# Order of the weight sums, the combine passes and the activation sums in the MLP stage of a decoder layer

## Chip, cores and metric

One core of one Trainium2 chip. The metric is the device time of one execution in microseconds (us), median of several runs. One launch computes the whole layer.

## What is computed

One layer of a hybrid decoder, in float32: an input projection, dilated window attention in three groups, a gated mixing of positions, an output projection with residual, and a squared-ReLU MLP. All that the change touches lies in the MLP, on N = 512 + 32 = 544 token columns, with D = 2048 and an inner width of 8192:

```python
h2 = rms_norm(x, norm_ffn)
x = x + jnp.square(jax.nn.relu(h2 @ w_up)) @ w_down
```

## The kernel before

Activations are kept transposed, features on the 128 partitions and tokens along the free axis; NH = 272 is half of the tokens. Every float32 operand is split into a high part (a cast to the matmul's float32 type, on ScalarE, ACT) and a low part (the difference, on VectorE, DVE), and a product is three matmuls: high times high, high times low, low times high (L903 to L905, on TensorE, PE).

The MLP's products are done by a scheme of Strassen's kind: a 2 × 2 block product with seven block products for eight. It needs sums of four weight blocks ahead of the matmuls, sums of four activation blocks likewise, and a combination of the seven results behind them.

**Units and stretches.** The MLP is a loop over 256 units (L888), 128 of `w_up` and then 128 of `w_down`. A unit is one weight load of 512 KB (`raw`, three buffers, issued on SyncE's queue, SP) and 42 matmuls of 272 columns: seven products × two halves j × three. Four units (g = 0 to 3) accumulate into the same seven PSUM tiles `qs[1]` to `qs[7]`; they make a stretch s, of which there are 32 up and 32 down. `qs[1]` and `qs[2]` lie in one tile `pt` (`pa`), `qs[6]` and `qs[7]` in another (`pb`), the rest in one each. The products of a unit go in the order 1, 2, 6, 7, 5, 4, 3.

**What a unit issues, in program order** (L888 to L907): the load of the raw weights of unit u+3; `prepare()` (L721) for unit u+1; the hooks of (s, g); its own 42 matmuls; and in g = 3 the end of the stretch. Each engine runs its instructions in that order.

**prepare** makes the sums `vs` (L733 two blocks, L735 and L736 one each, every one from the one before), casts the raw blocks and the sums to `vh` (ACT: L732 and L737) and makes the differences `vl` (DVE: L738 and L739). `vs`, `vh` and `vl` have two buffers each, so the casts for unit u+1 wait until PE has left unit u−1.

**End of a stretch.** `combine` (L763) copies `qs[1]` to SBUF (ACT, L765) and makes four results out of the seven tiles in seven DVE passes (L766 to L772). PE's first matmul of the next stretch overwrites `qs[1]`.

**Up** (`up_out`, L818): the result tile `f` gets a ReLU and a square on ACT in g = 1 of the next stretch (L823, L824), then in g = 2 its three sums (`sums`, L682: L683 to L685) and a store to DRAM `rd` by GpSimd's queue (POOL, L828).

**Down** (`down_out`, L859): the results go by an accumulating DMA to DRAM `yd` (POOL, L864). In g = 1 of each down stretch one activation tile of the following stretches is loaded from `rd` into `tl` (POOL, L838), in g = 2 it is split (`down_terms`: ACT L843, DVE L844). Around the turn from up to down, in stretches 31 and 32, nine such tiles are loaded and split. In the last eight stretches the finished sums are loaded, scaled (L848) and stored. `scale_back` (stretches 2 to 4) makes row factors, among them two reciprocals; in eight up stretches (8, 10, .. 22) L813 scales a part of the residual into `yd`.

Of the kernel before, what the change touches and what calls it, by code (L numbers as in the profile page):

```python
# [23 lines left out]
N = NP_ + NS  # L24
NH = N // 2
# [13 lines left out]
VB = 2 * P  # L39
# [4 lines left out]
def halves(t):  # L44
    return t.rearrange("p (a b) -> p a b", a=2)
# [7 lines left out]
def hybrid_layer_kernel(ctx, tc, xT, w_in, w_out, w_up, w_down, kc1, kc23, vc1, vc23, gains, biasp,  # L53
                        biass, gw, gws, gb, consts, y, kout, vout, gvout):
    nc = tc.nc
    V, A, G, S = nc.vector, nc.scalar, nc.gpsimd, nc.sync
# [12 lines left out]
    def load(src):  # L69
        raw = wp.tile([P, 8, P], F32, name="raw", bufs=3)  # L70
        S.dma_start(out=raw, in_=src)
        return raw

    def split_half(raw, j, copy=A.copy):
        wh = sp.tile([P, 4, P], F32R, name="wh", bufs=AHEAD + 1)
        wl = sp.tile([P, 4, P], F32R, name="wl", bufs=AHEAD + 1)
        r = raw[:, 4 * j:4 * j + 4, :]
        copy(wh, r)  # L78
        V.tensor_tensor(wl, r, wh.bitcast(F32), op=OP.subtract)  # L79
        return wh, wl  # L80
# [80 lines left out]
    def vtile():  # L161
        return ap.tile([P, N], F32, name="v", bufs=2)
# [7 lines left out]
    ssq = ap.tile([P, N], F32, name="ssq", tag="ss")  # L170

    pts = [main_psum() for _ in range(2)]
    raws = {}
# [26 lines left out]
    for c in range(4):  # L200
# [5 lines left out]
        w1 = split_half(raws[1, c // 2], c % 2, copy=V.tensor_copy)  # L206
# [29 lines left out]
    def quad(dst, src):  # L236
        for a in range(4):
            for b in range(4):
                G.tensor_copy(dst[32 * a:32 * a + 32, b:b + 1], src[32 * b:32 * b + 32, a:a + 1])
# [6 lines left out]
    class Head:  # L246
# [260 lines left out]
    i = 0  # L507
    for h in range(NHEAD):
# [9 lines left out]
        for g in range(NG):  # L518
            pt = in_tile(i)
            i += 1  # L520
            t = vtile()
# [96 lines left out]
    ssq = vtile()  # L618
# [7 lines left out]
    for f in range(4):  # L626
        pt = in_tile(i)
        i += 1
        u = vtile() if f == 2 else zt[4 + f % 2]
# [5 lines left out]
    for part in range(2):  # L635
        if part:
            plan.drain()
        for pt in pts:
            if not part:
                plan.step()  # L640
            w = stream.get(load, split_half)
# [13 lines left out]
    ssq = tp.tile([P, N], F32, name="ssq1")  # L655
# [25 lines left out]

    def sums(f):  # L682
        V.tensor_tensor(f[:, 0:2, :], f[:, 7:8, :].to_broadcast([P, 2, NH]), f[:, 4:7:2, :], op=OP.subtract)  # L683
        V.tensor_tensor(f[:, 2, :], f[:, 6, :], f[:, 0, :], op=OP.subtract)
        V.tensor_tensor(f[:, 3, :], f[:, 5, :], f[:, 2, :], op=OP.subtract)  # L685

    def split_terms(k, f):
# [3 lines left out]
    def terms(k):  # L691
        f = xp.tile([P, 8, NH], F32, name="f")
        for dst, m in ((f[:, 4:8:3, :], k), (f[:, 5:7, :], k + PAIRS)):
            V.scalar_tensor_tensor(dst, halves(x1[m]), gn[:, 16 + m:17 + m], halves(rb), op0=OP.mult, op1=OP.mult)
        sums(f)
        split_terms(k, f)

    for m in M_ORDER[:2]:
# [14 lines left out]
    mix.close()  # L713

    uw = ctx.enter_context(tc.tile_pool(name="uw", bufs=1, side="right", reuse_waits="tile"))
    raws = []

    def fetch(src):
        raws.append(load(src))

    def prepare():  # L721
        raw = raws.pop(0).rearrange("p a b -> p (a b)")
        vs = uw.tile([P, 4 * VB], F32, name="vs", bufs=2)
        vh, vl = (uw.tile([P, 7 * VB], F32R, name=n, tag=n, bufs=2) for n in ("vh", "vl"))

        def part(t, i):
            return t[:, i * VB:(i + 1) * VB]

        def pair(t):
            return t.rearrange("p (a b) -> p a b", a=2)  # L730

        A.copy(vh[:, :3 * VB], raw[:, VB:])  # L732
        V.tensor_tensor(pair(vs[:, :2 * VB]), raw[:, None, :VB].to_broadcast([P, 2, VB]), pair(raw[:, VB:3 * VB]),  # L733
                        op=OP.add)
        V.tensor_tensor(part(vs, 2), part(vs, 1), part(raw, 1), op=OP.add)  # L735
        V.tensor_tensor(part(vs, 3), part(vs, 2), part(raw, 3), op=OP.add)  # L736
        A.copy(vh[:, 3 * VB:], vs)  # L737
        V.tensor_tensor(vl[:, :3 * VB], raw[:, VB:], vh[:, :3 * VB].bitcast(F32), op=OP.subtract)  # L738
        V.tensor_tensor(vl[:, 3 * VB:], vs, vh[:, 3 * VB:].bitcast(F32), op=OP.subtract)  # L739
        return vh, vl  # L740

    th.append(uw.tile([P, 7, NH], F32R, name="th7", tag="th7"))
    tl.append(uw.tile([P, 7, NH], F32R, name="tl7", tag="tl7"))
    units = [w[i] for w in (w_up, w_down) for i in range(w.shape[0])]
    for i in range(3):
        fetch(units[i])
    ready = [prepare()]
    terms(PAIRS - 1)
    tmp.close()
    yp = ctx.enter_context(tc.tile_pool(name="yp", bufs=1, reuse_waits="tile"))  # L750
# [3 lines left out]
    qs = {n: t[:, :NH] for n, t in ((1, pa[:, 0]), (2, pa[:, 1]), (6, pb[:, 0]), (7, pb[:, 1]), (5, q5), (4, q4),  # L754
                                     (3, q3))}
# [5 lines left out]
        return yp.tile([P, 8, NH], F32, name="f", bufs=2)  # L761

    def combine(c11, c12, c21, c22):  # L763
        w = yp.tile([P, NH], F32, name="w", bufs=2)
        A.copy(w, qs[1])  # L765
        V.tensor_tensor(c11, qs[2], w, op=OP.add)  # L766
        V.tensor_tensor(w, qs[6], w, op=OP.subtract)
        V.tensor_tensor(c21, qs[7], w, op=OP.add)
        V.tensor_tensor(w, qs[5], w, op=OP.add)
        V.tensor_tensor(c22, qs[5], c21, op=OP.add)  # L770
        V.tensor_tensor(c21, qs[4], c21, op=OP.add)
        V.tensor_tensor(c12, qs[3], w, op=OP.subtract)  # L772

    hooks = {}

    def hook(s, g, fn, *args):
        hooks.setdefault((s, g), []).append(partial(fn, *args))

    back = yp.tile([P, N], F32, name="back")

    def scale_back():
        o = out_tile()
# [35 lines left out]
    def up_out(p):  # L818
        f = term_tile()
        combine(f[:, 4, :], f[:, 7, :], f[:, 5, :], f[:, 6, :])  # L820

        def square():
            A.activation(f[:, 4:, :], f[:, 4:, :], AF.Relu)  # L823
            A.activation(f[:, 4:, :], f[:, 4:, :], AF.Square)  # L824

        def rest():
            sums(f)
            G.dma_start(out=rd[p], in_=f[:, :7, :])  # L828

        hook(p + 1, 1, square)  # L830
        hook(p + 1, 2, rest)

    def load_terms(n):
        k = n % PAIRS
# [42 lines left out]
    last, first = UPG - 1, UPG  # L877
# [9 lines left out]

    for u in range(len(units)):  # L888
        s, g = divmod(u, 4)
        if u + 3 < len(units):  # L890
            fetch(units[u + 3])
        if u + 1 < len(units):
            ready.append(prepare())
        for fn in hooks.get((s, g), []):
            fn()
        vh, vl = ready.pop(0)
        t0 = max(s - UPG, 0)
        for n, (v, t) in TERMS.items():
            for j in range(2):
                k = (t0 + 2 * g + j) % PAIRS  # L900
                c = slice(v * VB + j * P, v * VB + (j + 1) * P)
                first, last = g + j == 0, g + j == 4
                mm(qs[n], vh[:, c], th[k][:, t, :], start=first, stop=False)  # L903
                mm(qs[n], vh[:, c], tl[k][:, t, :], start=False, stop=False)  # L904
                mm(qs[n], vl[:, c], th[k][:, t, :], start=False, stop=last)  # L905
        if g == 3:
            up_out(s) if s < UPG else down_out(s - UPG)  # L907
# [198 lines left out]
```

## Time and profile before

| | us |
|---|---|
| median of 3 runs | 2199.11 |
| lowest and highest run | 2193.5, 2201.91 |
| profiled execution, device time | 2193.06 |
| span of its trace | 2191.3 |
| busy in the span: PE | 2096.3 (96%) |
| busy: DVE | 1754.9 (80%) |
| busy: ACT | 929.9 (42%) |
| busy: POOL | 234.5 (11%) |

The span goes from the first to the last instruction of one profiled execution. Matmuls overlap, and one is busy until its modelled end, so a share of PE near 100% means a gapless stream. The mean granted clock of TensorE is 0.987 of full speed. An arrow in a row names what ended an engine's idle time ahead of an instruction.

### The profile page before, as it was taken

Reading aid. Unit: us, or ns where it says so; the run is one execution under the profiler, and the core shown is the slowest. Engines: PE = TensorE matmul, PEld = TensorE weight load, DVE = VectorE, ACT = ScalarE, POOL = GpSimd, SP = SyncE. Lnnn points to the kernel's source line nnn. Section 1 sums busy time; section 2 is a strip of 40 time slices with the busy share of each in tenths; the row PEclk is TensorE's granted clock in tenths of the full one; section 3 lists DMA queues with packets and bytes.
Section 4 is the critical chain, followed back from the end, with each engine's and each line's share of the span. In section 5 each row is a group of like instructions: output and inputs, shape, how many; then the busy total and the mean of one; then the engine's idle time right before and its main releaser. Section 6 shows DMA issues by size and latency. Waiting matters only on the chain.

```text
span 2191.3 us, 40901 instructions
## 1 busy us (share of the span) xinstructions
PE 2096.3 (96%) x16392; PEld 2063.7 (94%) x16392; DVE 1754.9 (80%) x3566; ACT 929.9 (42%) x1296; POOL 234.5 (11%) x534
## 2 busy tenths in 40 slices
PE   8999999999899889999999999998999999999997
PEld 8999989899898889999999999998999999999997
DVE  5356767666687779989999998889888888898997
ACT  5334242332633344444444444455444444444442
POOL 3121120211211100000000000010000000000111
PEclk9999999999999999999999999999999999999999
DMA  5365665656564424454554544464655555565665
GB/s 190 97 192 185 209 194 190 207 181 197 179 200 131 158 94 150 145 170 165 179 179 163 181 154 148 159 261 140 185 152 182 153 181 168 173 181 155 205 212 156
DMA packets 109695, 378.13 MB, mean 173 GB/s; under 512 B 12640, under 2 KB 12752, under 8 KB 109504
## 3 DMA queue, kind: packets, MB, share of 16 engines
q1 hardware_dynamic: 81744, 243.58, 34.2%
q0 software_dynamic: 27760, 131.94, 19.7%
q8 instruction: 128, 2.10, 0.4%
q14 instruction: 63, 0.52, 0.1%
HBM read 305.87 MB, written 69.21 MB: 171 GB/s over the span
## 4 chain that ended last, share of the span: by engine, by line
PE 47%; issue 31%; DVE 8%; DMA 7%; ACT 3%; POOL 2%; SPq 0%; POOLq 0%; DVEq 0%; ACTq 0%
PE pt L87 14%; PE pt L903 6%; PE pt L905 6%; PE pt L904 6%; DMA kv<-in_kc_dram 4%; PE sm L903 2%; PE po L903 2%; PE sm L904 2%; PE po L904 2%; PE sm L905 2%; PE ms L904 2%; PE ms L903 2%; PE ms L905 2%; PE po L905 1%; POOL yd L864 1%
## 5 line engine op out<-in xcount | busy, mean ns | idle before, releaser
L903 PE MATMUL pt<-th,vh 128*128 128x272 f32 x2048 | 598.7, 292 | 23.3 <-DVE o L766 15.5
L904 PE MATMUL pt<-tl,vh 128*128 128x272 f32 x2048 | 595.0, 291 | 7.3 <-DVE tl L844 7.3
L905 PE MATMUL pt<-th,vl 128*128 128x272 f32 x2048 | 594.5, 290 | 5.2 <-DVE vl L738 5.2
L737 ACT CAST vh<-vs 128x1024 fp32r<-128x1024 f32 x256 | 269.5, 1053 | 401.3 <-DVE vs L736 400.0
L903 PEld LDWEIGHTS pt<-th,vh 128*128 128x128 f32 x2048 | 389.5, 190 | 30.6 <-DVE o L766 20.6
L904 PEld LDWEIGHTS pt<-tl,vh 128*128 128x128 f32 x2048 | 389.8, 190 | 8.4 <-DVE tl L844 8.4
L905 PEld LDWEIGHTS pt<-th,vl 128*128 128x128 f32 x2048 | 390.7, 191 | 5.7 <-DVE vl L738 5.7
L732 ACT CAST vh<-raw 128x768 fp32r<-128x768 f32 x256 | 213.8, 835 | 345.3 <-PE po L904 205.9
L739 DVE TENSOR_TENSOR vl<-vs,vh 128x1024 fp32r<-128x1024 f32 x256 | 313.9, 1226 | 54.1 <-ACT vh L737 53.8
L87 PE MATMUL pt<-hh,wh 128*128 128x272 f32 x1408 | 303.9, 298 | 6.0 <-DVE wh L78 6.0
L87 PE MATMUL pt<-hh,wl 128*128 128x272 f32 x1408 | 295.6, 292 | 1.4 <-DVE wl L79 1.4
L87 PE MATMUL pt<-hl,wh 128*128 128x272 f32 x1408 | 295.6, 292 | 0.5 <-DVE hl L183 0.5
L738 DVE TENSOR_TENSOR vl<-raw,vh 128x768 fp32r<-128x768 f32 x256 | 243.9, 953 | 22.5 <-ACT vh L732 21.1
L87 PEld LDWEIGHTS pt<-hh,wh 128*128 128x128 f32 x1408 | 224.9, 193 | 17.0 <-issue 8.2
L79 DVE TENSOR_TENSOR wl<-raw,wh 128x512 fp32r<-128x512 f32 x208 | 144.1, 699 | 107.6 <-ACT wh L78 106.6
L87 PEld LDWEIGHTS pt<-hl,wh 128*128 128x128 f32 x1408 | 226.1, 193 | 0.9 <-DVE hl L183 0.9
L87 PEld LDWEIGHTS pt<-hh,wl 128*128 128x128 f32 x1408 | 225.0, 193 | 1.6 <-DVE wl L79 1.6
L78 ACT CAST wh<-raw 128x512 fp32r<-128x512 f32 x200 | 121.3, 616 | 154.0 <-PE pt L87 137.8
L733 DVE TENSOR_TENSOR vs<-raw 128x512 f32<-128x512 f32 x256 | 175.1, 684 | 0.0
L903 PE MATMUL po<-th,vh 128*128 128x272 f32 x512 | 148.1, 289 | 0.0
L903 PE MATMUL sm<-th,vh 128*128 128x272 f32 x512 | 147.7, 289 | 0.0
L903 PE MATMUL ms<-th,vh 128*128 128x272 f32 x512 | 147.6, 288 | 0.0
(233 smaller groups left out, 3772.9 us busy)
## 6 DMA issues: line engine op xcount, KB each, us to landing
raw<-in_w_up_dram SPq DMA_DIRECT2D x128, 512.0 KB
raw<-in_w_down_dram SPq DMA_DIRECT2D x128, 512.0 KB
raw<-in_w_in_dram SPq DMA_DIRECT2D x84, 512.0 KB
tl<-rd POOLq DMA_DIRECT2D x39, 952.0 KB, 7.9
rd<-f POOLq DMA_DIRECT2D x32, 952.0 KB, 4.3
kv<-in_kc_dram SPq DMA_DIRECT2D x96, 256.0 KB
kv<-in_vc_dram SPq DMA_DIRECT2D x96, 256.0 KB
yd<-o POOLq DMA_DIRECT2D x39, 544.0 KB, 5.5
```

The lines of the kernel that those rows point to most:

```text
L78: copy(wh, r)
L79: V.tensor_tensor(wl, r, wh.bitcast(F32), op=OP.subtract)
L87: mm(pt[:, c, :NH], wt[:, j, :], at[:, c * NH:(c + 1) * NH], start=start and n == 0, stop=stop and n == 2)
L732: A.copy(vh[:, :3 * VB], raw[:, VB:])
L733: V.tensor_tensor(pair(vs[:, :2 * VB]), raw[:, None, :VB].to_broadcast([P, 2, VB]), pair(raw[:, VB:3 * VB]), op=OP.add)
L737: A.copy(vh[:, 3 * VB:], vs)
L738: V.tensor_tensor(vl[:, :3 * VB], raw[:, VB:], vh[:, :3 * VB].bitcast(F32), op=OP.subtract)
L739: V.tensor_tensor(vl[:, 3 * VB:], vs, vh[:, 3 * VB:].bitcast(F32), op=OP.subtract)
L864: G.dma_start(out=yd[q], in_=o, accum_op=OP.add)
L903: mm(qs[n], vh[:, c], th[k][:, t, :], start=first, stop=False)
L904: mm(qs[n], vh[:, c], tl[k][:, t, :], start=False, stop=False)
L905: mm(qs[n], vl[:, c], th[k][:, t, :], start=False, stop=last)
```

## The change

Four things change, all in the MLP.

1. `prepare` is cut in two: `sum_weights(u)` makes the sums, `split_weights(u)` the casts and differences. In unit u the sums of unit u+2 are made (the first two passes ahead of the split of unit u+1, the last one behind it), so that the split of u+1 finds its sums ready.
2. `combine` has a tile of three slices for its intermediate results (two in use by turns and one, `x`, for what was written into `c21`), and another order of the passes: `w2` from `qs[6]` first, then `c11` from `qs[2]`, and so on.
3. The three passes of `sums` of an up stretch are spread: one in g = 2 and one in g = 3 of the next stretch, the last, with the store to `rd`, in g = 0 of the one after.
4. The tile `back` is the tile `ssq`.

```diff
     def sums(f):
         V.tensor_tensor(f[:, 0:2, :], f[:, 7:8, :].to_broadcast([P, 2, NH]), f[:, 4:7:2, :], op=OP.subtract)
+        yield
         V.tensor_tensor(f[:, 2, :], f[:, 6, :], f[:, 0, :], op=OP.subtract)
+        yield
         V.tensor_tensor(f[:, 3, :], f[:, 5, :], f[:, 2, :], op=OP.subtract)
...
-        sums(f)
+        list(sums(f))
         split_terms(k, f)
...
-        A.copy(vh[:, :3 * VB], raw[:, VB:])
+    def sum_weights(u):
+        raw = raws[u]
+        vs = summed[u] = uw.tile([P, 4 * VB], F32, name="vs", bufs=2)
         V.tensor_tensor(pair(vs[:, :2 * VB]), raw[:, None, :VB].to_broadcast([P, 2, VB]), pair(raw[:, VB:3 * VB]),
                         op=OP.add)
         V.tensor_tensor(part(vs, 2), part(vs, 1), part(raw, 1), op=OP.add)
+        yield
         V.tensor_tensor(part(vs, 3), part(vs, 2), part(raw, 3), op=OP.add)
+        yield
+
+    def split_weights(u):
+        raw, vs = raws[u], summed[u]
+        vh, vl = (uw.tile([P, 7 * VB], F32R, name=n, tag=n, bufs=2) for n in ("vh", "vl"))
+        A.copy(vh[:, :3 * VB], raw[:, VB:])
         A.copy(vh[:, 3 * VB:], vs)
         V.tensor_tensor(vl[:, :3 * VB], raw[:, VB:], vh[:, :3 * VB].bitcast(F32), op=OP.subtract)
         V.tensor_tensor(vl[:, 3 * VB:], vs, vh[:, 3 * VB:].bitcast(F32), op=OP.subtract)
-        return vh, vl
+        ready[u] = vh, vl
...
-    ready = [prepare()]
+        fetch(i)
+    list(sum_weights(0))
+    split_weights(0)
+    list(sum_weights(1))
     terms(PAIRS - 1)
...
     def combine(c11, c12, c21, c22):
-        w = yp.tile([P, NH], F32, name="w", bufs=2)
-        A.copy(w, qs[1])
-        V.tensor_tensor(c11, qs[2], w, op=OP.add)
-        V.tensor_tensor(w, qs[6], w, op=OP.subtract)
-        V.tensor_tensor(c21, qs[7], w, op=OP.add)
-        V.tensor_tensor(w, qs[5], w, op=OP.add)
-        V.tensor_tensor(c22, qs[5], c21, op=OP.add)
-        V.tensor_tensor(c21, qs[4], c21, op=OP.add)
-        V.tensor_tensor(c12, qs[3], w, op=OP.subtract)
+        w = yp.tile([P, 3, NH], F32, name="w")
+        w1, w2, w3, x = (w[:, i, :] for i in (0, 1, 0, 2))
+        A.copy(w1, qs[1])
+        V.tensor_tensor(w2, qs[6], w1, op=OP.subtract)
+        V.tensor_tensor(c11, qs[2], w1, op=OP.add)
+        V.tensor_tensor(x, qs[7], w2, op=OP.add)
+        V.tensor_tensor(w3, qs[5], w2, op=OP.add)
+        V.tensor_tensor(c22, qs[5], x, op=OP.add)
+        V.tensor_tensor(c21, qs[4], x, op=OP.add)
+        V.tensor_tensor(c12, qs[3], w3, op=OP.subtract)
...
-    back = yp.tile([P, N], F32, name="back")
+    back = ssq
...
-        def rest():
-            sums(f)
+        parts = sums(f)
+        hook(p + 1, 1, square)
+        hook(p + 1, 2, partial(next, parts))
+        hook(p + 1, 3, partial(next, parts))
+
+        def last():
+            next(parts, None)
             G.dma_start(out=rd[p], in_=f[:, :7, :])
 
-        hook(p + 1, 1, square)
-        hook(p + 1, 2, rest)
+        hook(p + 2, 0, last)
...
-        if u + 3 < len(units):
-            fetch(units[u + 3])
+        fetch(u + 3)
+        sums_next = sum_weights(u + 2) if u + 2 < len(units) else iter(())
+        next(sums_next, None)
         if u + 1 < len(units):
-            ready.append(prepare())
+            split_weights(u + 1)
+        next(sums_next, None)
         for fn in hooks.get((s, g), []):
             fn()
-        vh, vl = ready.pop(0)
+        vh, vl = ready.pop(u)
```

## Rows read from the trace of the kernel before

**Rows 1.** Busy us by stage; columns PE, PEld, DVE, ACT, POOL, clock, DMA, GB/s.

```profile
778.60:809.10 30.50, 24.90 (x168) 24.24 (x169) 24.93 (x37) 10.25 (x12) 0.00 (x0) 0.89 0.30 95
809.10:896.60 87.50, 85.67 (x678) 84.63 (x676) 78.82 (x125) 40.34 (x46) 2.68 (x5) 1.00 0.40 136
896.60:1445.50 548.90, 548.87 (x4368) 548.87 (x4369) 496.19 (x792) 254.99 (x285) 24.32 (x45) 1.00 0.49 165
1445.50:1506.40 60.90, 48.77 (x338) 47.04 (x336) 54.74 (x66) 35.35 (x32) 5.80 (x11) 0.92 0.64 246
1506.40:2159.00 652.60, 638.58 (x5040) 633.24 (x5041) 580.25 (x845) 286.69 (x300) 49.26 (x71) 1.00 0.59 177
```

**Rows 2.** Waits of PE in the whole span: total us, times, longest.

```profile
PE pt L903 <- DVE o L766: 15.5, 17, 1.9
...
PE pt L904 <- DVE tl L844: 7.3, 5, 1.8
...
PE pt L905 <- DVE vl L738: 5.2, 2, 3.3
```

**Rows 3.** Timeline of DVE, end of stretch 60 and next unit: start, length, instruction.

```profile
2090.11 1.23 DVE L739 TENSOR_TENSOR vl<-vs,vh 128x1024 fp32r<-128x1024 f32 x1 [0.24 <-ACT vh L737]
2091.25 0.43 DVE L766 TENSOR_TENSOR o<-pt,w 128x272 f32<-128x272 f32 x1
2091.79 0.44 DVE L767 TENSOR_TENSOR w<-pt,w 128x272 f32<-128x272 f32 x1
...
2092.81 0.44 DVE L769 TENSOR_TENSOR w<-sm,w 128x272 f32<-128x272 f32 x1
2093.16 0.43 DVE L770 TENSOR_TENSOR o<-sm,o 128x272 f32<-128x272 f32 x1
...
2094.41 0.68 DVE L733 TENSOR_TENSOR vs<-raw 128x512 f32<-128x512 f32 x1
2095.12 0.42 DVE L735 TENSOR_TENSOR vs<-vs,raw 128x256 f32<-128x256 f32 x1
2095.58 0.43 DVE L736 TENSOR_TENSOR vs<-vs,raw 128x256 f32<-128x256 f32 x1
2095.92 0.95 DVE L738 TENSOR_TENSOR vl<-raw,vh 128x768 fp32r<-128x768 f32 x1
...
2098.27 0.69 DVE L733 TENSOR_TENSOR vs<-raw 128x512 f32<-128x512 f32 x1
```

**Rows 4.** Timeline of PE at the same boundary.

```profile
2090.26 0.29 PE L905 MATMUL po<-th,vl 128*128 128x272 f32 x1
2091.74 0.39 PE L903 MATMUL pt<-th,vh 128*128 128x272 f32 x1 [1.19 <-DVE o L766]
```

**Rows 5.** DMA issues from 1550 to 2150: count, size, median us to landing.

```profile
tl<-rd POOLq DMA_DIRECT2D x28, 952.0 KB, 7.8
...
o<-yd POOLq DMA_DIRECT2D x6, 544.0 KB, 6.6
out_y_dram<-o POOLq DMA_DIRECT2D x5, 544.0 KB, 4.4
```

**Rows 6.** Timelines of POOL, ACT and DVE in stretch 45.

```profile
1769.03 0.86 POOL L864 DMA_DIRECT2D yd<-o  x1 [18.80 <-DVE o L772]
1771.31 0.55 POOL L838 DMA_DIRECT2D tl<-rd  x1 [1.43 <-PE po L904]
...
1779.61 1.78 ACT L843 CAST th<-tl 128x1904 fp32r<-128x1904 f32 x1 [0.55 <-DMA tl<-rd]
...
1781.42 2.14 DVE L844 TENSOR_TENSOR tl<-tl,th 128x1904 fp32r<-128x1904 f32 x1 [1.11 <-ACT th L843]
```

**Rows 7.** Timelines of ACT and DVE in the last unit of up stretch 20.

```profile
1229.24 0.84 ACT L732 CAST vh<-raw 128x768 fp32r<-128x768 f32 x1 [3.49 <-PE po L904]
...
1232.38 1.29 DVE L813 TENSOR_TENSOR o<-o,back 128x1088 f32<-128x1088 f32 x1
1233.58 0.43 DVE L766 TENSOR_TENSOR f<-pt,w 128x272 f32<-128x272 f32 x1
```

More of the change, by code (lines that the diff above doesn't have):

```diff
@@ L715, in hybrid_layer_kernel, with fetch, part, pair @@
     uw = ctx.enter_context(tc.tile_pool(name="uw", bufs=1, side="right", reuse_waits="tile"))
[L716 to L730, printed above, removed]
-        A.copy(vh[:, :3 * VB], raw[:, VB:])
+    raws, summed, ready = {}, {}, {}
+    def fetch(u):
+        if u < len(units):
+            raws[u] = load(units[u]).rearrange("p a b -> p (a b)")
+    def part(t, i):
+        return t[:, i * VB:(i + 1) * VB]
+    def pair(t):
+        return t.rearrange("p (a b) -> p a b", a=2)
+    def sum_weights(u):
+        raw = raws[u]
+        vs = summed[u] = uw.tile([P, 4 * VB], F32, name="vs", bufs=2)
         V.tensor_tensor(pair(vs[:, :2 * VB]), raw[:, None, :VB].to_broadcast([P, 2, VB]), pair(raw[:, VB:3 * VB]),
@@ L745, in hybrid_layer_kernel @@
     for i in range(3):
-        fetch(units[i])
-    ready = [prepare()]
+        fetch(i)
+    list(sum_weights(0))
+    split_weights(0)
+    list(sum_weights(1))
     terms(PAIRS - 1)
```

## Prediction

> **What bounds the kernel now.** I read the busy time by stage first, then the waits of TensorE, then single stretches on the timeline. The stages of [rows 1] are: the first stretch, stretches 1 to 4, 5 to 30, 31 and 32, and 33 to 62. In 5 to 30 PE is busy for 548.87 of 548.90 us: 26 stretches of 168 matmuls, 21.11 us each, 5.28 a unit. That is the pace at which nothing can be gained. Elsewhere the excess over that pace is the most that any edit of the other engines can bring: 30.5 − 21.1 = 9.4 in the first stretch, 87.5 − 84.4 = 3.1 in 1 to 4, 60.9 − 42.2 = 18.7 in 31 and 32, and 652.6 − 633.3 = 19.3 in 33 to 62; in all 50.5.
>
> [rows 2] say who is late: PE's first matmul of a stretch waits for DVE's L766 (the pass that reads `qs[2]`; 17 times, 15.5 us), in the turn from up to down 7.3 us for `tl` from L844, and for 5.2 us, most of it in the first stretch, for `vl` from L738. So it is DVE, and its order of work, that costs PE time, although DVE is 89% busy in 33 to 62 and PE 98%.
>
> [rows 3] show why. They are DVE in a stretch end and the unit after it. A pass whose successor reads or overwrites what it handled holds that successor until it has ended: L766 to L767 is 0.54 from start to start for a pass of 0.43, L735 to L736 0.46 for 0.42. A pass whose successor is free of it lets it start early: L769 to L770 0.35 (0.44 long), L736 to L738 0.34, L739 (1.23) to its successor 1.14. The `combine` lasts 3.16 (2091.25 to 2094.41), one unit of weights 3.86 (2094.41 to 2098.27), 0.24 of it a wait of L739 for ACT's cast L737, which waits for the sums of the same unit. A down stretch is then 4 × 3.86 + 3.16 + 2.06 (L844) + 0.45 (its wait for ACT) = 21.1: DVE has exactly PE's pace, and all that comes on top (L848 1.20 in the last ones, a late `tl`) is lost. [rows 4] show one: PE's last matmul of the stretch starts at 2090.26, the next at 1.48 later, 0.06 after L766's end.
>
> **The change part by part.** Times are start to start.
>
> *Weights.* A unit on DVE becomes L733 0.72 (the pass that reads its sum still follows it), L735 0.34 (L738 is now free of it), L738 0.86 (0.95 less the 0.09 by which L739's successor starts early; an estimate from that row, upper end 1.20, today's), L739 1.14, the last sum 0.34: 3.40 for 3.86. ACT's L737 no longer waits for sums. Each `raw` is needed one unit (5.28) sooner. SP's queue is unchanged: the load is still released by L738 of the unit three before. The distance from that release to L733 falls from about two units plus 1.5 to one unit plus 1.5, 6.8 us. The trace gives no landing time for a `raw`; nearest are transfers of 544 KB in 4.4 and 6.6 and of 952 KB in 7.8 [rows 5], so 512 KB take 4.4 to 7.8. I take 5.5 (the size is that of the first two), and nothing for it: L738 can't run before ACT's cast, which waits for PE to leave the other `vh`, so DVE has idle time ahead of it. In a down stretch the load released at 3.0 (first unit) is due for the third: landed at 11.3 it would have L844 start at 14.7 and PE released at 14.7 + 2.06 + 3.40 + 0.35 + 0.43 = 20.9 of 21.1. So up to 8.3 is hidden.
>
> *Combine.* Seven passes at 0.35 make 2.45 for 3.16. But L766's successor of the same work, `c11`, now stands second, behind `w2`, so PE's release comes 0.35 later in the order.
>
> *Down stretches, 33 to 62.* The weights and the combine give back 4 × 0.46 + 0.71 = 2.55 and the wait for ACT 0.45, so DVE needs 18.2 of 21.1 and is bound by arrivals. The one that ends last is `tl` [rows 6]. There the stretch began at 1765.97 (the `tl` load is issued 0.06 after the end of its first unit, 1771.25) and ended at 1787.07. `tl` landed at 1779.6, ACT's L843 took 1.78, L844 began at 1781.42, and 2.06 + 3.86 + 0.43 later, at 1787.77, PE was released: 0.7 late. With the same landing the changed kernel gives 1781.42 + 2.06 + 3.40 + 0.35 + 0.43 = 1787.66: only 0.1 is saved. What moves the landing is Pool's queue: `yd` stands ahead of `tl` in it and is issued 0.31 after the combine's last pass, at 3.06 into the stretch. With `c11` ending before the boundary, the last pass waits only for the last matmul (about 0.5 in, after the others 0.7), ends at 1.15, and `yd` goes at 1.5. If `tl` follows by as much, it lands near 1778.0, L843 starts behind L737 at 1778.4, L844 at 1780.2, PE's release is due at 1786.45, 0.6 before PE wants it. No stall, as long as `tl` lands within 12.95 of the stretch's start, 7.6 after issue; the median is 7.8 [rows 5], less up to 1.5. L848 falls into DVE's idle time of the second unit (it has 1.2, before L738 of the third, which waits for PE). I keep 0.1 a stretch, 3 us: −16.3. Ends: −19.3 (nothing left) and −5.5 (landings as now, so that 15.5 − 17 × 0.1 = 13.8 stay).
>
> *Turn, 31 and 32.* Both are a string of DVE work: nine L844 at 2.06. In 32 the four units save 1.84, the combine 0.71, four waits of L844 for ACT 1.8 (ACT now has the casts done early), the three passes of `sums`, spread over three units, about 0.5 of held time: −4.9. In 31, where L844 is fixed by PE and ACT, a pass L684 and `w2` now stand ahead of `c11`: +0.7. Ends −6 and 0.
>
> *First stretch.* The sums of unit 1 (0.72 + 0.46 + 0.34) go ahead of `terms`, those of unit 2 up to L735 (1.06) ahead of unit 1's L738, which lost its own 1.52: `vl` of unit 1 is 1.06 later, and PE waits for it: +1.1. Stretches 1 to 4: reciprocals of 1.8 us now have more passes behind them ahead of `c11`, but DVE catches up sooner; 0, ends −2 and +1.5.
>
> *Up stretches.* Unit 3 ends with L739, the last sum, L684, `w2`, `c11`. In the stretch of [rows 7] the unit began at 1234.4 − 5.28 = 1229.16 (boundary: 896.6 + 16 × 21.11 = 1234.4), ACT's L732 at 1229.24 and L739 at 1232.38 − 1.14 = 1231.24, 2.08 into it; without ACT's wait for the sums I take 1.95. `c11` then ends at 1.95 + 1.14 + 0.34 + 0.35 + 0.35 + 0.43 = 4.56 of 5.28: hidden by 0.7; with no cover the three passes cost 1.04 a stretch. In eight of them, as in this one, L813 (1.20) stands there too: it moves from 1232.38 to about 1232.6, `c11` to 1234.5, ending 1234.93, where PE wants it at 1234.4; now it ends at 1234.01. So 0.55 × 8 = +4.4, ends 0 and +8.
>
> *Moved at no cost:* the DMA of `rd` goes from the third unit to the first of the next stretch, on Pool ahead of nothing urgent (a `rd` is read many stretches later, its `f` is written again only at that stretch's end); in the turn the store of 29 moves just ahead of the first `tl` loads and that of 30 from amid them to behind the eighth: the queue's total is the same, and DVE's nine L844 are the bound there, not the landings; `back` shares `ssq`, which is last read before the first write of `back`. The last combine: −0.5 (0.71 less, but its last pass waits for PE; ends −0.7 and 0).
>
> Sum: 1.1 + 0 + 4.4 − 4.2 − 16.3 − 0.5 = −15.5. The profiled execution took 2193.06 (span 2191.3 and 1.8 around it), so 2177.6. It lies 6 below the median of the runs, near their lowest; on the median the sum gives 2183.6. I put 2181.
>
> A rule speaks against the edit: the Trainium skill (VectorE: DVE Perf Modes, "The DRAIN you can't avoid") says that after every DVE pass the pipe empties before the next starts, that semaphores cost nothing extra there, and that one should lower the number of passes, not of waits. By it the reordering would bring little but ACT's wait; the time is that of rival 2. The 0.35 against 0.54 of [rows 3] disagrees with it, and so does a later section of the same page ("Two Vector instructions with no wait between them"), by which a pass that isn't held starts earlier.
>
> **The rivals.** (1) *`tl` stays the bound*: its landing doesn't follow `yd`, because the two `raw` loads that are issued earlier now run beside it. For it: those loads share the DMA engines; against: the whole pattern moves together. Down then gives −5.5, in all −4.7: 2188 on the profiled run, 2194 on the median.
> (2) *The passes still wait for each other* (each holds its successor whatever it reads, or the waits are kept by whole tiles: PE's first matmul, which writes one half of `pt`, does wait for a reader of the other). Then the combine stays 3.16, a unit is 3.73, `c11` second costs 0.54, the L813 stretches lose 1.0 each, down keeps about 9, the turn gives −1.9: 1.2 + 8 − 10.3 − 1.9 = −3: 2190, or 2196 on the median. Against it: L770 does start 0.09 before L769 has ended.
> (3) *Slower: loads come late.* With `raw` due one unit sooner, in the down stretch the load released in the first unit, beside `yd` and `tl`, is late for L733 of the third. From about 8.3 on, each us of landing is a us of PE in each of 30 stretches. At 9.2 the gain is gone and 11 more lost (0.9 × 30 = 27); at 9.5 it is 2214. [rows 5] speak against it (4.4 to 7.8), that it shares its time with the two longest transfers for it.
>
> **How the numbers follow.** Forecast 0.66, rival 1 0.17, rival 2 0.09, rival 3 0.08. The forecast's own range is 2172 to 2188 (ends of the up and the down term on either base). The range has to reach rivals 1 and 2: 2168 to 2196. A measurement of this kernel tells 0.5%, 11 us, from no change: faster is below 2188 and holds most of the forecast and little else, 0.67; rivals 1, 2 and the forecast's upper end make same 0.24; slower is rival 3, 0.09.
>
> **What would show it.** Right: a unit of weights on DVE near 3.4 and a combine near 2.45; PE's waits for L766's successor in 33 to 62 down from 15.5 to some 3; L844 starting by 14.3 into the stretch with `yd` issued near 1.5; new waits of about 0.5 in eight up stretches. Wrong: `tl` landing as late as now (rival 1), passes at 0.54 (rival 2), L733 waiting for the DMA of `raw` (rival 3), or waits for `c11` in ordinary up stretches.

## Result, and the profile after

The changed kernel took 2186.52 us (median; 2181.28 to 2194.46) beside 2198.74 for the kernel before: a ratio of 0.9947 with a 95% interval from 0.9934 to 0.9960, or −12.2 us. The prediction's sum on the median was 2183.6, the number put down 2181, the range 2168 to 2196. Measured a second time, on another chip (e10 below), it gave 0.9970 (0.9956 to 0.9985). Both intervals lie below 1: the kernel is faster, by something between 0.15% and 0.66%.

The code ahead of the MLP is the same in every kernel here, yet the MLP's first matmul starts between 778.6 and 786.2 in the profiles. So the kernels are compared from that matmul on. The table gives, in us, the time from the first matmul of a part to the first of the next (read from TensorE's timeline); the last column runs from the first matmul of the MLP to the end of the span.

| | first | 1–4 | 5–30 | 31 | 32 | 33–62 | 63, tail | MLP |
|---|---|---|---|---|---|---|---|---|
| before | 30.5 | 87.5 | 548.9 | 24.2 | 36.8 | 652.6 | 32.3 | 1412.6 |
| before again (e8) | 30.6 | 87.5 | 548.8 | 24.2 | 36.7 | 651.8 | 32.1 | 1411.8 |
| after | 32.6 | 86.6 | 553.7 | 26.8 | 31.7 | 640.2 | 31.6 | 1403.2 |
| after again (e10) | 32.2 | 86.5 | 553.7 | 26.5 | 31.7 | 642.6 | 31.6 | 1404.9 |
| e1 sums alone | 31.7 | 86.1 | 548.8 | 24.0 | 32.7 | 647.3 | 31.7 | 1402.4 |
| e2 combine alone | 30.6 | 87.2 | 549.9 | 24.6 | 36.0 | 648.3 | 31.7 | 1408.4 |
| e3 store early | 32.6 | 87.3 | 550.9 | 24.5 | 32.0 | 640.0 | 31.6 | 1398.9 |
| e4 `c11` first | 32.6 | 85.9 | 550.6 | 26.5 | 31.9 | 641.4 | 31.6 | 1400.4 |
| e5 `yd` behind `tl` | 30.6 | 87.5 | 548.9 | 24.2 | 36.7 | 644.5 | 38.1 | 1410.5 |
| e6 four mends | 30.6 | 86.1 | 548.9 | 24.0 | 32.1 | 639.1 | 31.6 | 1392.3 |
| e7 e6, `yd` behind | 30.6 | 86.1 | 548.9 | 24.0 | 32.1 | 633.0 | 37.8 | 1392.5 |
| e9 `yd` behind to 55 | 30.6 | 86.1 | 548.9 | 24.0 | 32.1 | 631.7 | 31.6 | 1384.9 |

By the profiles the change saves 7 to 9 us in the MLP, where the prediction summed up 15.5. The views of after that answer to [rows 1 to 3, 5] follow; in its lines L733, L735 and L737 are the sums of the weights, L745 and L746 the differences, L776 to L782 the combine (L776 is `w2`, L777 `c11`), L843 the store to `rd`, L852 the load of `tl`, L857 and L858 its split, L878 the DMA to `yd`, L919 to L921 the matmuls.

Busy time by stage of the changed kernel:

```profile
781.70:814.30 32.60, 25.96 (x169) 25.30 (x170) 25.75 (x41) 10.14 (x11) 0.00 (x0) 0.84 0.27 89
814.30:900.90 86.60, 85.64 (x679) 84.67 (x678) 75.14 (x126) 38.66 (x45) 4.15 (x7) 1.00 0.42 136
900.90:1454.50 553.60, 550.31 (x4370) 548.79 (x4369) 471.14 (x791) 248.50 (x286) 22.33 (x42) 1.00 0.48 162
1454.50:1513.10 58.60, 46.81 (x339) 45.34 (x337) 52.84 (x68) 36.03 (x33) 5.79 (x11) 0.94 0.67 255
1513.10:2153.30 640.20, 632.86 (x5040) 631.88 (x5041) 560.29 (x849) 272.47 (x298) 49.91 (x72) 1.00 0.60 182
```

Against [rows 1] the third number of each row after the length, DVE's busy time, fell in every stage but the first (580.25 to 560.29 in 33 to 62), though the work is the same: the passes are as many, but they overlap. The up stretches (third row) became 4.7 longer.

Its waits of TensorE, whole span:

```profile
PE pt L919 <- DVE o L777: 9.5, 5, 2.9
PE pt L919 <- DVE f L777: 8.8, 9, 5.5
```

L777 takes the place of L766 in [rows 2]. At the ends of down stretches (`o`) 17 waits became five, but long ones. Of the nine at the ends of up stretches (`f`) eight are new, in the stretches with L813; the ninth, in stretch 31, is 5.5, where the kernel before had 2.9.

DVE at the end of down stretch 45 and in the next unit:

```profile
1790.43 0.68 DVE L733 TENSOR_TENSOR vs<-raw 128x512 f32<-128x512 f32 x1
1791.15 0.42 DVE L735 TENSOR_TENSOR vs<-vs,raw 128x256 f32<-128x256 f32 x1
1791.50 0.95 DVE L745 TENSOR_TENSOR vl<-raw,vh 128x768 fp32r<-128x768 f32 x1
1792.36 1.22 DVE L746 TENSOR_TENSOR vl<-vs,vh 128x1024 fp32r<-128x1024 f32 x1
1793.50 0.42 DVE L737 TENSOR_TENSOR vs<-vs,raw 128x256 f32<-128x256 f32 x1
1793.84 0.43 DVE L776 TENSOR_TENSOR w<-pt,w 128x272 f32<-128x272 f32 x1
1794.19 0.43 DVE L777 TENSOR_TENSOR o<-pt,w 128x272 f32<-128x272 f32 x1
...
1795.92 0.43 DVE L782 TENSOR_TENSOR o<-po,w 128x272 f32<-128x272 f32 x1
1796.27 0.68 DVE L733 TENSOR_TENSOR vs<-raw 128x512 f32<-128x512 f32 x1
```

From L733 to L776 the unit lasts 3.41 (forecast 3.40, before 3.86), from L776 to the next L733 the combine lasts 2.43 (forecast 2.45, before 3.16), with 0.35 from pass to pass. L746 no longer waits for ACT.

POOL's queue at that boundary (the stretch begins at 1795.27), and the DMA issues from 1550 to 2150:

```profile
1796.66 0.86 POOL L878 DMA_DIRECT2D yd<-o  x1 [16.64 <-DVE o L782]
1800.51 0.55 POOL L852 DMA_DIRECT2D tl<-rd  x1 [3.00 <-PE po L920]
```

```profile
tl<-rd POOLq DMA_DIRECT2D x28, 952.0 KB, 6.7
...
o<-yd POOLq DMA_DIRECT2D x6, 544.0 KB, 6.2
```

`yd` is issued 1.39 into the stretch (before 3.06), `tl` as before at 5.24, and `tl` lands in 6.7 for 7.8 [rows 5].

### The profile page after: what moved, and what is told of

It reads as the page before. It is cut to its first block, busy times and chain, and to the rows that moved or that the text cites. A ratio compares the mean times of both kernels' runs of the same rounds, so it can differ in the third digit from the quotient of the medians.

```text
span 2184.9 us, 41096 instructions
## 1 busy us (share of the span) xinstructions
PE 2091.5 (96%) x16392; PEld 2062.1 (94%) x16392; DVE 1702.2 (78%) x3566; ACT 908.5 (42%) x1296; POOL 234.4 (11%) x534
## 4 chain that ended last, share of the span: by engine, by line
PE 57%; issue 22%; DMA 9%; DVE 8%; ACT 3%; POOL 1%; SPq 0%; POOLq 0%; DVEq 0%; ACTq 0%
PE pt L919 9%; PE pt L921 9%; PE pt L87 9%; PE pt L920 9%; DMA kv<-in_kc_dram 4%; PE sm L919 2%; PE po L919 2%; PE sm L920 2%; PE sm L921 2%; PE po L920 2%; PE ms L920 2%; PE ms L919 2%; PE ms L921 2%; PE po L921 2%; DMA fb<-fr 1%
## 5 line engine op out<-in xcount | busy, mean ns | idle before, releaser
L919 PE MATMUL pt<-th,vh 128*128 128x272 f32 x2048 | 595.1, 291 | 23.4 <-DVE o L777 9.5
L921 PE MATMUL pt<-th,vl 128*128 128x272 f32 x2048 | 593.2, 290 | 4.8 <-DVE vl L745 4.8
L919 PEld LDWEIGHTS pt<-th,vh 128*128 128x128 f32 x2048 | 388.4, 190 | 27.6 <-issue 11.9
L921 PEld LDWEIGHTS pt<-th,vl 128*128 128x128 f32 x2048 | 389.5, 190 | 5.2 <-DVE vl L745 5.2
L745 DVE TENSOR_TENSOR vl<-raw,vh 128x768 fp32r<-128x768 f32 x256 | 244.7, 956 | 153.1 <-ACT vh L743 153.1
L746 DVE TENSOR_TENSOR vl<-vs,vh 128x1024 fp32r<-128x1024 f32 x256 | 313.0, 1223 | 0.3 <-ACT vh L744 0.2
L733 DVE TENSOR_TENSOR vs<-raw 128x512 f32<-128x512 f32 x256 | 175.4, 685 | 8.7 <-DMA raw<-in_w_down_dram 7.7
L919 PE MATMUL po<-th,vh 128*128 128x272 f32 x512 | 147.9, 289 | 0.0
L919 PE MATMUL sm<-th,vh 128*128 128x272 f32 x512 | 147.7, 288 | 0.0
L919 PE MATMUL ms<-th,vh 128*128 128x272 f32 x512 | 147.4, 288 | 0.0
```

## Experiments

**e1 and e2: one part each.** e1 is the kernel before with part 1 of the diff (weights' sums) alone, e2 with part 2 (combine, and `back` in `ssq`) alone.

> The kernel before with part 1 of the change alone (weights' sums one unit ahead); old combine, old sums and store. Theory A (the down stretches are bound by arrivals, and what counts is how early the last combine pass lets yd, and with it tl, be issued): a unit 3.40 and the combine still 3.16 on VectorE; without the 0.46 of each unit the combine begins before the boundary, so yd is issued near 1.9 into the stretch instead of 3.1 and most of the down gain is there: 33 to 62 lose 8 to 11 us; stretch 32 about -3.5, stretch 31 0 to +1 (no store ahead of the tl loads), first stretch +2 (as in the changed kernel), the eight stretches with L813 nothing. In all -8 to -12 against the kernel before. Rival B (the reordered combine brings the down gain): 33 to 62 lose 3 or less, in all -3 to 0.

> The kernel before with part 2 of the change alone (three slices and the new order in the combine; the row factors' tile shared). Theory A: combine 2.45 with 0.35 from pass to pass, units still 3.86. yd is issued 0.7 earlier, tl lands so much earlier, but c11 comes 0.35 later in the order: 33 to 62 lose 3 to 7 us; the eight L813 stretches 0 to +0.3 each (c11 had 0.43 of cover), turn -0.7 to -1.5. In all -3 to -8. Rival B (the combine's order is the source of the gain): -9 to -12. Rival C (passes wait for each other whatever they read): combine still 3.16, passes at 0.45, in all 0 to +3.

Measured against the kernel before: e1 0.9945 (0.9931 to 0.9959), e2 0.9965 (0.9951 to 0.9979); in the MLP −10.3 and −4.2. In 33 to 62 they save 5.2 and 4.3, together 9.5, and both at once, in the changed kernel, 12.3 (10.0 in its second profile). So neither part carries it alone. That both at once save more than the sum is not shown: in e1 TensorE runs two of these stretches, 33 and 45, without a gap but in part at its lower clock (1.2 GHz of 2.4; the mean granted clock, third number from the end, is 0.92 and 0.93), and so some 2.9 over its pace of 21.11:

```profile
1509.48:1532.12 22.64, 22.64 (x169) 22.61 (x169) 18.84 (x28) 7.42 (x8) 1.46 (x2) 0.92 0.50 145
1770.62:1793.14 22.52, 22.52 (x168) 22.52 (x169) 19.69 (x30) 8.00 (x9) 1.41 (x2) 0.93 0.58 179
```

The first profiles of the kernel before and of the changed one have nothing of this in 33 to 62; e2 lost 1.1 by it in 33. Without it e1 would have saved about 8 here (an estimate from these rows), the lower end of the 8 to 11 expected, and e2 about 5.4. In the total e1's −8 to −12 came, with −4.0 from stretch 32. Two expectations failed: `yd` was not issued near 1.9 in e1, and the turn of e2 saved 0.3 and not 0.7 to 1.5. What held `yd` back in e1 its trace shows. DVE of e1 at an ordinary boundary (here L773 is `c11`, L774 to L779 the other passes, L851 the split of `tl`), then its POOL queue and its `tl` loads:

```profile
1850.55 2.14 DVE L851 TENSOR_TENSOR tl<-tl,th 128x1904 fp32r<-128x1904 f32 x1 [1.26 <-ACT th L850]
...
1856.01 0.43 DVE L773 TENSOR_TENSOR o<-pt,w 128x272 f32<-128x272 f32 x1
1856.55 0.44 DVE L774 TENSOR_TENSOR w<-pt,w 128x272 f32<-128x272 f32 x1
...
1858.82 0.43 DVE L779 TENSOR_TENSOR o<-po,w 128x272 f32<-128x272 f32 x1
```

```profile
1859.55 0.86 POOL L871 DMA_DIRECT2D yd<-o  x1 [18.50 <-DVE o L779]
```

```profile
tl<-rd POOLq DMA_DIRECT2D x28, 952.0 KB, 8.2
```

DVE idles 1.26 for `tl`, so `c11` ends as the stretch ends, and the six passes behind it still take 0.44 each on the mean: `yd` goes 3.05 into the stretch, as before (3.05 is the median of its down stretches too), and `tl` is late again. The lateness feeds itself. `tl` even lands 0.4 later than before (8.2 for 7.8), with the `raw` loads of the stretch issued sooner (4.6 and 8.0 into stretch 40, for 5.2 and 9.0). In e2 the six passes take 0.35 each:

```profile
1858.38 0.43 DVE L768 TENSOR_TENSOR o<-pt,w 128x272 f32<-128x272 f32 x1
...
1860.12 0.43 DVE L773 TENSOR_TENSOR o<-po,w 128x272 f32<-128x272 f32 x1
```

```profile
tl<-rd POOLq DMA_DIRECT2D x28, 952.0 KB, 6.9
```

Here L768 is `c11` and L773 the last pass: even after a late `c11` `yd` goes 1.89 into the stretch, and `tl` lands 0.9 sooner. With both parts (the changed kernel, stretches 44 to 46) one late stretch, at 2.96, is followed by one at 1.89, and that by 1.38: the loss heals instead of repeating.

**e3: part 3 undone.** The changed kernel with the three activation sums and the store where they were:

```diff
-        hook(p + 1, 2, partial(next, parts))
-        hook(p + 1, 3, partial(next, parts))
-        def last():
-            next(parts, None)
+        def rest():
+            list(sums(f))
             G.dma_start(out=rd[p], in_=f[:, :7, :])
-        hook(p + 2, 0, last)
+        hook(p + 1, 2, rest)
```

> The changed kernel with part 3 undone: all three activation sums and the store to rd in the third unit of the next stretch, as in the kernel before. Theory A (the store of 29 right ahead of the first tl loads, and that of 31 right ahead of the tl load of stretch 33, make those loads and the raw load beside them late): stretch 31 from 26.8 to 24.2 to 25, stretch 33 from 24.1 to 21.1 to 21.4; besides, without the pass L684 ahead of c11 the eight L813 stretches wait 0.2 instead of 0.57 (-2.7 in all); stretch 32 0 to +0.5. In all 6 to 8 us below the changed kernel. Rival B (the raw load, needed one unit sooner, and chance in the landings are the cause, not the store): stretch 31 stays at 26 to 27 or 33 at 23 to 24; in all only 2 to 4 below the changed kernel.

Measured 0.9929 of the kernel before (0.9917 to 0.9941), in the MLP 4.3 below the changed kernel for the 6 to 8 expected; the rest was missing in stretch 33 (below). The eight L813 stretches wait 0.22 each for 0.57, as expected. Stretch 31 falls from 26.8 to 24.5. POOL's queue there and DVE's late pass in the changed kernel:

```profile
1459.78 0.53 POOL L843 DMA_DIRECT2D rd<-f  x1 [20.57 <-issue]
1460.31 1.06 POOL L852 DMA_DIRECT2D tl<-rd  x2
```

```profile
1472.54 0.69 DVE L733 TENSOR_TENSOR vs<-raw 128x512 f32<-128x512 f32 x1 [3.35 <-DMA raw<-in_w_down_dram]
```

and POOL's and DVE's in e3 (L838 is the store, L848 the load):

```profile
1448.13 0.53 POOL L838 DMA_DIRECT2D rd<-f  x1 [20.57 <-issue]
1458.35 1.06 POOL L848 DMA_DIRECT2D tl<-rd  x2 [9.68 <-PE po L916]
```

```profile
1468.63 0.68 DVE L733 TENSOR_TENSOR vs<-raw 128x512 f32<-128x512 f32 x1
```

With the store right ahead of two `tl` loads, the `raw` that comes beside them is late by 3.35 for a sum which now needs it one unit sooner; with the store ten us earlier the same pass starts 15.5 into the stretch instead of 18.0 and waits for nothing. That `raw` load is issued at the same place in both kernels, 7.25 into the stretch: it took 10.7 us beside the store, and had landed within 8.3 without it. That is rival 3's mechanism, at one place.

In stretch 33 the changed kernel has the same picture (POOL, then ACT, stretch from 1513.08):

```profile
1518.97 0.56 POOL L843 DMA_DIRECT2D rd<-f  x1 [3.10 <-issue]
1519.52 0.54 POOL L852 DMA_DIRECT2D tl<-rd  x1
```

```profile
1528.99 1.78 ACT L857 CAST th<-tl 128x1904 fp32r<-128x1904 f32 x1 [3.44 <-DMA tl<-rd]
```

`tl` lands 9.4 after its issue, DVE's split waits for ACT's cast of it for 3.67, and TensorE waits 3.06 at the stretch's end. In e3 that wait is gone, but stretch 33 was only 0.3 shorter, for another reason, seen in its busy time and TensorE's timeline:

```profile
1509.55:1533.40 23.85, 23.85 (x169) 23.85 (x170) 18.86 (x31) 7.31 (x8) 1.46 (x2) 0.87 0.53 151
```

```profile
1510.36 0.43 PE L915 MATMUL pt<-th,vh 128*128 128x272 f32 x1
1510.59 0.43 PE L916 MATMUL pt<-tl,vh 128*128 128x272 f32 x1
```

TensorE never stops there, but its first matmuls start 0.23 apart for 0.125 elsewhere: the granted clock was at its lower level (1.2 GHz of 2.4; the mean of the stretch is 0.87), behind a turn in which it had idled for 10 us. Neither profile of the changed kernel has it in 33; e1, e2, e3, e6, e7 and the second profile of the kernel before do (1.1 to 2.6 us), so it is not the edit's. In 33 to 62 the lower clock stands in other places too, each time in the stretch behind a wait of 2 us or more: in 45 behind 44 in e1 (above), e4 and e6, in 41 behind 40 in e10, 1.2 to 1.5 us each.

**e4: `c11` first.** The changed kernel with L776 and L777 exchanged.

> The changed kernel with c11 (the pass that reads the tile that TensorE overwrites first) ahead of w2 in the combine, as in the order of the kernel before. Theory A: TensorE is released one pass, 0.35, sooner wherever it waits for this pass: the eight L813 stretches wait 0.22 instead of 0.57 (-2.8 in all), stretch 31 -0.35; the pass x is now held by w2 right ahead of it, 0.1 to 0.2 in each combine, hidden. In all 2 to 4 us below the changed kernel. Rival B (the pair of passes is held in either order, or the wait of TensorE is for the whole tile pair): within 1 us of the changed kernel.

Measured 0.9927 (0.9912 to 0.9942), in the MLP 2.8 below the changed kernel: each of the eight L813 costs 0.22 for 0.57 (0.13 in its own stretch and 0.1 in the next), stretch 31 is 0.34 shorter. Theory A holds. The pass `x` then follows `w2` at 0.46 instead of 0.35 (read in e6, which has the same order), and `yd` goes 0.13 later (1.51 for 1.38), which costs nothing.

**e5: `yd` behind `tl`, in the kernel before.**

```diff
-            G.dma_start(out=yd[q], in_=o, accum_op=OP.add)
+            hook(UPG + t + 1, 1, lambda: G.dma_start(out=yd[q], in_=o, accum_op=OP.add))
```

> The kernel before with one edit: the accumulating DMA to yd of a down stretch is issued in the second unit of the next stretch, behind the tl load, instead of ahead of it. Nothing is saved on VectorE. Theory A (in the down stretches PE waits because tl lands late, and tl lands late because yd stands ahead of it in Pool's queue): the tl load still goes at 5.3 into the stretch, lands in about 5 instead of 7.8, VectorE's split starts 2 earlier, and nearly all waits of PE for L766 in stretches 33 to 57 go, those of 58 to 62 in part: 33 to 62 from 652.6 to between 636 and 643, in all 10 to 16 below the kernel before. Rival B (tl shares the DMA engines with whatever else runs, above all the loads of raw, and the order in Pool's queue does not matter): landing still 7 or more, 33 to 62 within 4 of 652.6.

Its `tl` loads, and TensorE's waits in 33 to 62:

```profile
tl<-rd POOLq DMA_DIRECT2D x28, 952.0 KB, 6.7
```

```profile
PE pt L903 <- DVE o L766: 7.8, 7, 1.8
```

With nothing saved on DVE, the order of two issues takes 8.0 us out of 33 to 62, and all but three of the late arrivals (44, 45, 48: 2.1 us) go; what stays are the five stretches 58 to 62 with L848, 6.3 us, where DVE itself has too much to do. So of the 17 us that the kernel before lost there about 11 were arrivals and 6 DVE's own time. The forecast of 636 to 643 was missed by 1.5, less than these five stretches lose. `tl` fell to 6.7 and not to 5; that it shares the DMA engines with the `raw` loads would explain it, but no run here shows it alone. In the whole the kernel gained little, if anything, 0.9988 (0.9976 to 1.0): the last stretch and the tail grew by 5.8.

**e6: four mends of the changed kernel.** Part 3 undone (e3), `c11` first (e4), L813 with its DMA one unit later, and at the MLP's start the sums of unit 1 behind `terms` and those of unit 2 behind the split of unit 1.

```diff
-    list(sum_weights(1))
     terms(PAIRS - 1)
+    list(sum_weights(1))
...
-        hook(8 + 2 * q, 3, rest)
+        hook(9 + 2 * q, 0, rest)
...
-        next(sums_next, None)
+        if u > 0:
+            next(sums_next, None)
         if u + 1 < len(units):
             split_weights(u + 1)
-        next(sums_next, None)
+        list(sums_next)
```

> The changed kernel with four places mended where it lost against the sum: part 3 undone (store and activation sums as before), c11 ahead of w2, the pass L813 with its DMA one unit later (first unit of the next stretch), and the sums of unit 1 behind terms, those of unit 2 behind the split of unit 1 in the first unit. Theory: first stretch from 32.6 to 30.5 to 31; stretches 5 to 30 from 553.7 to 549; stretch 31 from 26.8 to 24.1 (store 2.3, c11 0.35); stretch 33 without a gap (21.1, up to 2.6 more if TensorE's clock is granted at half for its first matmuls, as in the run with the store early); 34 to 62 unchanged. In all 8 to 13 below the changed kernel, 0.988 to 0.991 of the kernel before. Rival: L813 ahead of another stretch's work only moves the wait (5 to 30 stay above 551) and the first stretch is bound by its raw loads (32): 4 to 6 below the changed kernel.

Measured 2173.47 us, 0.9901 (0.9886 to 0.9916); in the MLP 10.9 below the changed kernel. Every stage came out as expected: the first 30.6, 5 to 30 at 548.9 without a gap, 31 at 24.0. Stretches 33 and 45 are 1.5 over the pace at the lower clock. In 33 to 62 two stretches with a long wait are left, 40 and 44, 2.1 each.

**e7 and e9: `yd` behind `tl` on top of it**, in e7 in every down stretch, in e9 in the first 24 only.

> The kernel with the four mends, and yd issued behind tl as well. Theory A: the four to five stretches that still wait (35, 38, 40, 41, 44) wait for tl behind yd; with tl ahead of it they go: 33 to 62 from 640 to 633 to 636, 4 to 6 below the kernel with the four mends. Rival B (those late landings have another cause, a late issue on Pool's queue or a collision with raw): 33 to 62 at 638 to 641, no difference.

> The kernel with the four mends, yd issued behind tl in the first 24 down stretches and ahead of it, as before, in the last eight, where the finished sums are loaded back. Theory: with yd behind tl everywhere, stretches 33 to 62 took 633.0 for 639.1, but the part behind the last matmul took 16.9 for 10.7, since the last yd, the load of its sums and the last store follow each other in one queue. So 33 to 62 at 633 to 635 and the tail at 10.7: 5 to 7 below the kernel with the four mends, 2166 to 2169. Rival (the tail grew because the sums of all earlier yd land later, not for the last one): tail still above 14, no gain.

e7: 33 to 62 fell to 633.0, no stretch waits at its end, and `tl` lands in 5.7. Of the 6.1 us gained there on e6, 4.2 are the waits of 40 and 44, and 1.6 are stretch 45, which has the full clock again. In all 0.9907 (0.9891 to 0.9922), no better than e6, as the tail grew by 6.2. Its POOL queue at the end (L874 is `yd`, L864 the load of the sums, L860 the store; the last stretch begins at 2139.76):

```profile
2150.74 0.94 POOL L874 DMA_DIRECT2D yd<-o  x1
2159.83 0.55 POOL L864 DMA_DIRECT2D o<-yd  x1 [8.16 <-DMA yd<-o]
```

The last `yd` goes 11 into the stretch, right behind a store that waited for DVE, and the load of its sums waits for it. In e9 it goes at once, and the down stretches are gapless (busy time of 33 to 62, TensorE 631.70 of 631.70):

```profile
1500.24:2131.94 631.70, 631.70 (x5040) 631.70 (x5041) 561.49 (x848) 271.88 (x298) 49.92 (x71) 1.00 0.62 183
```

e9 took 2171.41 us (2165.34 to 2174.38), 0.9882 (0.9862 to 0.9901), the fastest kernel here, 26 below the kernel before. The expected tail came, and 33 to 62 were shorter still, 1.3 of it because stretch 33 had the full clock here. The median missed the 2166 to 2169 expected. And between e6 and e9 the medians differ by 2 where the MLP of the two profiles differs by 7.4 (some 3 of it the lower clock of e6), and the intervals overlap, so how much the last step is worth is not settled.

**e8 and e10: both kernels again.**

> The kernel before once more, for a second profile. Its first one lies 6 below the median of its runs. If that is chance in the landings of tl, 33 to 62 are above 652.6 here or in other runs by some us, with waits for L766 in other stretches than in the first profile; if it is chance ahead of the MLP, the MLP begins later than at 778.65 (in the other profiles 781.7 to 786.2) and 33 to 62 stay within 1.

> The changed kernel once more, beside it on the same chip, for a second profile. If the losses found are the kernel's own and not chance, they stand in the same places: eight up stretches 0.57 each, stretch 31 near 26.8, first stretch near 32.6, tl late in 40 and 44 (2 each); in 33 either 3 of gap or, in its place, first matmuls at half the granted clock. From the first matmul of the MLP to the end of the span 1401 to 1405 (1403.2 in the first profile; 1412.6 and 1411.8 in the two of the kernel before).

e8: the MLP begins at 783.06 and takes 1411.8, 0.8 less than in the first profile, with waits in partly other stretches. So the first profile of the kernel before was low ahead of the MLP, by chance. e10: the eight stretches, 31, 33, 40 and 44 lose in the same places, 0.57, 5.4, 2.4, 2.3 and 2.4; these losses are the kernel's own. 1404.9 is within what was expected. The two ratios of the changed kernel, 0.9947 and 0.9970, differ by 5 us. The start of the MLP differs by up to 7.6 between the profiles, but the ratios are of medians over at least 12 executions each: why they differ stays open.

## Why the prediction was right, and where it was wrong

The mechanism was right: the passes overlap, a unit and the combine have the lengths forecast, `yd` moved by 1.67, `tl` followed by 1.1, and the kernel is faster, by less than the sum said. That the first series came within 3 us of the sum on the median is in part luck: its −12.2 is more than either profile shows in the MLP, and the second series gave −7.6. Term by term (forecast, then the two profiles of the changed kernel, each against the first of the kernel before):

| term | forecast | first profile | second |
|---|---|---|---|
| first stretch | +1.1 | +2.1 | +1.7 |
| stretches 1 to 4 | 0 | −0.9 | −1.0 |
| up, 5 to 30 | +4.4 | +4.8 | +4.8 |
| turn, 31 | +0.7 | +2.6 | +2.3 |
| turn, 32 | −4.9 | −5.0 | −5.0 |
| down, 33 to 62 | −16.3 | −12.3 | −10.0 |
| end | −0.5 | −0.7 | −0.7 |
| sum | −15.5 | −9.5 | −7.8 |

*"Moved at no cost: the DMA of `rd`."* This step failed: it put at nothing what cost some 5 us. The prediction saw that the store of 29 comes to lie just ahead of the first `tl` loads, and let it pass because DVE's nine splits are the bound of the turn. But the first sum behind it was not: its `raw` now shares the engines with three transfers of 952 KB. e3 measured it: 2.3 us in stretch 31. That the store of 31 stands ahead of the `tl` load of 33 was not seen at all: a wait of 3.06 there, 2.4 in the second profile. Without the store there (e3, e6, e9) the wait is gone; e9's stretch 33, at the full clock, took 21.15.

*Down.* Two terms were left out of the 0.1 a stretch: this store, and stretches 40 and 44, where POOL issues late (below); with them 3.06 + 2.50 + 1.90 = 7.5 of the 8.1 us of waits in these stretches are named. The ordinary ones, which the prediction put at 21.2, were a little shorter still: 21.01 to 21.18. In the second profile 1.4 more went to the lower clock in 41. (A slip without effect: DVE's need in a down stretch, 4 × 3.40 + 2.45 + 2.06, is 18.1 and not 18.2.) The step from `yd` to `tl` was right in direction and too large: `tl` took 6.7, 1.1 less for 1.67, where the prediction granted up to 1.5. e5 shows directly that the order in POOL's queue counts for the landing. In e1, with `yd` and `tl` issued as before and the `raw` loads earlier, `tl` lands 0.4 later: this points to rival 1's mechanism, at about a quarter of the 1.5.

*Turn, 31.* Of +2.6, 2.3 were the store (e3 24.5; it puts the three sums back as well, but what came late was a pass that waited for a DMA), and 0.34 the order of `w2` and `c11` (e4); together with e6 (24.0) this leaves nothing open.

*First stretch.* The term was right, though 2.1 stands in the table for its 1.1. TensorE's waits in unit 1, and the rest of that unit (busy time; TensorE's clock is the third number from the end), before (MLP from 778.65) and after (from 781.73):

```profile
788.20 0.39 PE L903 MATMUL pt<-th,vh 128*128 128x272 f32 x1 [0.32 <-ACT vh L732]
792.04 0.60 PE L905 MATMUL pt<-th,vl 128*128 128x272 f32 x1 [3.32 <-DVE vl L738]
792.03:798.56 6.53, 6.52 (x40) 6.52 (x41) 5.95 (x9) 1.95 (x3) 0.00 (x0) 0.76 0.47 148
```

```profile
792.80 0.39 PE L919 MATMUL pt<-th,vh 128*128 128x272 f32 x1 [1.84 <-ACT vh L743]
796.17 0.59 PE L921 MATMUL pt<-th,vl 128*128 128x272 f32 x1 [2.85 <-DVE vl L745]
796.17:803.73 7.56, 7.56 (x41) 7.56 (x41) 5.81 (x9) 1.05 (x1) 0.00 (x0) 0.64 0.42 142
```

`vl` of unit 1 releases TensorE 14.44 into the MLP for 13.38: later by 1.06, as forecast. The cast to `vh` moved more, by 1.52 (it stands behind the cast in `terms` in ACT's order), which the prediction did not follow; but `vl` is the arrival that ends last, so this cost nothing. The other 1.0 is clock: behind that wait TensorE ran at a mean of 0.64 for 0.76. In e1, with the same order of sums, the wait ends at 14.44 too, the rest of the unit takes 6.65 at a clock of 0.74, and the stretch grew by 1.2 only. Why the lower level reached further there in the changed kernel (in both profiles, and in e3 and e4) stays open. With the sums behind `terms` (e6) the wait ends at 13.38 again, and the stretch is 30.6.

*Up.* As forecast: eight stretches, 0.57 each for 0.55; that letting the pass that releases TensorE go second costs one pass (0.35) was shown by e4.

*The rivals.* Rival 2 fell: passes at 0.35, the combine at 2.43, and e2, which only reorders them, gains. Rival 3 came true at one place, in the turn; in 33 to 62 DVE's waits for `raw` add up to 4.3 us in nine places, none over 0.7.

The Trainium skill (VectorE: DVE Perf Modes, "The DRAIN you can't avoid") says that the next pass does not start until the pipe is empty; the same paragraph adds that a pass that is not held starts earlier. The trace agrees with the addition: 0.35 from start to start for passes of 0.43, and e2, which changes only order and buffers, gains by it.

## What to carry to other kernels

Order the passes of an in-order engine so that none touches what the one ahead of it handled, but let the pass that another engine waits for go first. When work moves in program order, follow each of its DMAs to its new neighbours in the queue: here a store moved by ten us cost about 5. Where one edit delays two arrivals, only the one that ends last counts. Before two stages are compared, look at the granted clock in each: here it hid 2.9 us of what one part saves. And where a loss feeds itself (a late load makes the stretch end late, which issues the next load late), ask first what the load stands behind: changing the order of two issues took half of it away without saving a single pass.

## What the runs showed of the hardware

POOL issues two of its DMAs late in every profile here, always the 195th and the 202nd in its order, whatever they are: the load of `tl` in stretch 40 and `yd` in 44 in most, `yd` in 40 and `tl` in 44 where their order is exchanged. In the kernel before, in the changed one, and in e7:

```profile
1748.67 0.86 POOL L864 DMA_DIRECT2D yd<-o  x1 [19.67 <-DVE vs L736]
```

```profile
1754.18 0.87 POOL L878 DMA_DIRECT2D yd<-o  x1 [18.21 <-DVE vs L735]
```

```profile
1662.43 0.86 POOL L874 DMA_DIRECT2D yd<-o  x1 [1.15 <-issue]
...
1746.21 0.55 POOL L848 DMA_DIRECT2D tl<-rd  x1 [20.82 <-issue]
```

They come 1.1 to 1.3 later than their like, and the trace shows nothing that they wait for: the `vs` named in the first two rows is only DVE's latest pass by then, and `yd` doesn't read it (the last combine pass had ended 1.58 earlier, for 0.31 elsewhere). The cause stays open. The kernel before lost 0.3 and 0.4 there, the changed one 2.5 and 1.9. In 44 `yd` then goes only 0.4 ahead of a `raw` load (0.8 in the kernel before) and takes 7.5 us for 5.5, with `tl` behind it at 9.5. So it is in all profiles with `yd` ahead of `tl`: 0.4 ahead of a `raw` load it takes 7.4 to 7.7 in 44 (the changed kernel, e1, e3, e4, e6), 0.8 ahead 5.7 to 5.9 (the kernel before, e2). With `yd` behind `tl` (e7, e9) the same late issue costs nothing.

TensorE's lower clock behind the turn moves about: 1.1 to 2.6 us in stretch 33 in six of the profiles, none in the others. With the same code it was there in one profile of the kernel before and not in the other.
